# Two-layer encoder trunk on one core: transposes two products behind, a second tile in the attention stream, weight sums of two blocks on VectorE

## The chip, the cores and the metric

The kernel runs on one core of a Trainium2 chip. The metric is the device time of one execution in microseconds. Before the change it took 2719.93 us, the median of three runs (2718.82 to 2721.35).

## What is computed

Two layers over 1024 tokens of 1024 features. Layer 0 mixes tokens by neighbourhood attention, layer 1 by dense differential attention; both go on in the same way:

```python
o = mixer(rms_norm(x, g0))            # attention, then heads side by side
x = x + rms_norm(o @ w_o, g1)         # output projection, 1024 x 1024
u = rms_norm(x, g2) @ w_in            # 1024 x 5632
gate, val = jnp.split(u, 2, axis=-1)
gate = conv1d(gate, conv_w, width=3, per_feature=True) + conv_b
x = x + rms_norm((gelu(gate) * val) @ w_out, g3)
```

and each layer ends with a gated embedding that is added to x. In differential attention each head has two softmaxes, w = a0 - lam a1, and the head's output is normalised (`os` in the kernel) before w_o.

## The kernel before

**Products.** A float32 operand is split into a high part and a low part, each rounded for TensorE, and a product is three matmuls: high by high, high by low, low by high. The split of a loaded `raw` page into its parts is an activation on ScalarE (line 135) for the high part and a subtraction on VectorE (line 138) for the low one. A tile of 128 tokens times w_o is 8 steps over k, each 3 matmuls for each half of 512 columns: 48 matmuls of 128x512 (line 816).

**Order.** TensorE's instructions stand in the order in which the code emits them. The order of ScalarE, VectorE, GpSimd (POOL) and of the DMA queue on SyncE (SP) is made by a scheduler, except in a region from `mix_out`'s last product to the end of `first_three`, where ScalarE's and VectorE's order is the code's too. Each engine works strictly through its own list.

**The stream of layer 1.** `da` runs over 64 pairs of head and tile of queries: scores (line 637), softmax, turns of the weights (`da_turn`, line 659), values (`da_values`, line 673) and the output (`da_out`): the normalised `os` (line 679; a chain ScalarE line 676, VectorE line 677, POOL line 184, VectorE line 679) is transposed by one matmul (line 687). Between these steps `tick` lets a generator, `qkv_stream`, put in matmuls of other work: the qkv projections of later heads, then the first tile of the output projection (`first_out`, in two `pj` banks, k = 0 to 6, since k = 7 needs the last head). `last_rows` lays out the jobs that load and split w_o and the first tile's rows. `drain` runs what is left of the stream.

**`mix_out`.** Tiles go in the order 0, 4, 1, 5, 2, 3, 6, 7. For each: the product into one of two PSUM pages `m`; squares on ScalarE into the page `h` (line 956), the root on VectorE and POOL (lines 960, 184), the scaled residual (lines 966, 969), the norm (lines 179, 180, 192, into `h` again), and then on TensorE 8 transposes of `h` in two banks (line 203), which `put` copies and splits into the operand pages of the next stage. In iteration n TensorE has product n, then the transposes of tile n-1, written Tn-1 here (T0 to T7 by place in that order). The last product, T6, the first product of `gated` and T7 follow in the region; the last norm is line 1006.

**`gated`.** The product with w_in is made in 22 blocks of 128 features, each by a seven-product scheme on quarters: `one`, `six`, `two`, `five`, `three`, `four`, `seven`, 12 matmuls each. It needs four sums of the block's weight quarters (S1 to S4, `Block.sum`, line 1147, 128x512) and after the products sums out of PSUM on VectorE: `sum_u` (line 1174, must precede `three`, which goes on in the same bank), `upper` (line 1186, must precede `seven`), `sum_on`, `lower`. `c` is line 1180, ScalarE's copy, which must precede `four`; the second half of `upper` runs on POOL (line 1189). `taps` (line 1098), `gelu` and `mult` (line 1214, the two halves of c times v) end a block, and c and its sums are spilled to memory. Blocks 0 to 2 run in `first_three`, whose order is written by hand; from block 3 on the loop below it runs, with S1 to S4 on POOL.

**Who feeds whom.** SP issues all loads and spills in order; a load of weight quarters needs a free `raw` page (three), a spill needs its data.

Of the kernel before, what the change touches and what calls it, by code (L numbers as in the profile page):

```python
# [8 lines left out]
F32 = mybir.dt.float32  # L9
# [7 lines left out]
P = 128  # L17
D = 1024
SEQ = 1024
NT = SEQ // P  # L20
KT = D // P
# [5 lines left out]
D_HEADS = 8  # L27
FT = 22
PK = 2
EPS = 1e-6  # L30
LAMBDA_INIT = 0.8 - 0.6 * math.exp(-0.3)
RPITCH = 31
# [59 lines left out]
class Trunk:  # L92
# [229 lines left out]
    def qkv_stream(self, layer, hT, x, first, mid):  # L322
# [3 lines left out]
        W = self.i["qkv"][layer]  # L326
# [89 lines left out]
        self.last_rows(layer)  # L416
        yield from emb
        yield from self.first_out()

    def begin(self, stream):  # L420
        self.stream, self.qk, self.v, self.credit = stream, {}, {}, 0.0
# [276 lines left out]
    def da(self, hT, oT, first, mid):  # L698

        N = NT * D_HEADS  # L700
        with self.tc.tile_pool(name="xa1", bufs=2, reuse_waits="tile") as x, \
             self.psum("s", 2) as self.ps:
            self.begin(self.qkv_stream(1, hT, x, first, mid))
            self.chunk = {}
            self.need(self.qk, 0)
            self.da_scores(x, 0)
            self.tick(12 / 6)
            for n in range(N + 1):
                if n > 0:
                    self.need(self.v, (n - 1) // NT * 2 + 1)  # L710
                    self.da_values(x, n - 1)
                if n + 1 < N:
                    self.need(self.qk, (n + 1) // NT)
                    self.da_scores(x, n + 1)
                if n < N:
                    self.da_turn(x, n, 0)
                self.tick(0.34)
                if n < N:
                    self.da_turn(x, n, 1)
                self.tick(0.16)  # L720
                if n > 0:
                    self.da_out(x, n - 1, oT)
                self.tick(0.5)
            self.drain()

    def psum(self, name, bufs):
        return self.tc.tile_pool(name=self.uid("ps" + name), bufs=bufs, space=PSUM, reuse_waits="tile")
# [17 lines left out]
    def last_rows(self, layer):  # L745


        nc = self.nc
        src = self.i[("na_w_o", "da_w_o")[layer]]
        self.W, self.part0 = [], None  # L750
        page = lambda dt=F32R: self.page(self.r1, "r1", (P, 4, D), dt)
        pages = [page(), page(), page(F32)]
        raw = {}

        def load(kt):
            if kt < 4:
                raw[kt] = pages[2][:, kt]
            else:
                raw[kt] = self.page(self.raw, "raw")
            nc.sync.dma_start(raw[kt], src[kt * P : kt * P + P])  # L760

        def row(kt):
            if kt == 4:
                del pages[2]
                pages.extend([page(), page()])
            hi, lo = pages[2 * (kt // 4) : 2 * (kt // 4) + 2]
            parts = hi[:, kt % 4], lo[:, kt % 4]
            did = self.split(raw.pop(kt), *parts)
# [12 lines left out]
        for kt in range(6):  # L781
            load(kt)
        self.jobs += [lambda kt=kt: row(kt) for kt in range(6)] + [part, None] + [lambda kt=kt: row(kt) for kt in (6, 7)]

    def job(self, act, dve):

# [49 lines left out]
    def first_out(self):  # L836
# [9 lines left out]
        self.row(KT - 1)  # L846
        self.out0 = hi, lo, m

    def mix_out(self, layer, x_in, x1):


# [7 lines left out]
        with self.tc.tile_pool(name=f"xb{layer}", bufs=2, reuse_waits="tile") as x, self.psum("m", 2) as pm:  # L859
            W, last = self.W, self.opage  # L860
            order = (0, 4, 1, 5, 2, 3, 6, 7)
            b12, b21, b22 = (self.page(xl, k, (P, 4, 512)) for k in ("B12", "B21", "B22"))

            def load_x(t):
# [7 lines left out]
                return hi, lo, xi or load_x(t)  # L872

            with self.tc.manual_schedule(engines={ENG.SP}):
                second = self.out_part(layer, order[1])
                xs = [load_x(order[0])]
                g1 = self.bcast(x, "g1", self.i["norm_g"][layer, 1], bufs=1)
                xs.append(load_x(order[1]))
                g2 = self.bcast(x, "g2", self.i["norm_g"][layer, 2], bufs=1)
            hs = [self.page(x, "h"), self.page(x, "h")]  # L880
# [53 lines left out]
                        sum_t3(t), sum_t4(t, t2)  # L934
                return of_group

            def product_of(n, t):
                hi, lo, xi = ready.pop(0)
                part = [(hi[:, k], lo[:, k]) for k in range(KT)]
                h = hs[n] if n < 2 else self.page(x, "h")  # L940
                if n >= 2:
                    hs.append(h)
                if t == 0:
                    m = self.out0[2]
                    self.times(m, part[KT - 1 :], W[KT - 1 :], first=False)
                else:
                    m = pm.tile([P, D], F32, tag="m", name=self.uid("m"))
                    m = [m[:, :512], m[:, 512:]]
                    self.times(m, part, W)
                return m, h, xi  # L950

            def squares(m, h):
                ss = [self.col("ss"), self.col("sy")]
# [17 lines left out]

            ready = [load(*a) for a in zip(order, xs, (self.out0[:2], second))]
            for n, t in enumerate(order[:-1]):
                m, h, xi = product_of(n, t)
                residual(t, m, h, xi, root_of(squares(m, h)))
                self.normed(xi, h, g2)
                if n + 2 < NT:
                    ready.append(load(order[n + 2]))
                if n > 0:
                    self.transposed(hs[n - 1], put(order[n - 1], hs[n - 1]))  # L980
            gate = self.gate_begun(layer, X)

# [96 lines left out]
    def gated(self, layer, X, spill, spare):  # L1079
# [38 lines left out]
        with self.tc.tile_pool(name=f"xd{layer}", bufs=1, reuse_waits="tile") as y, self.psum("c", 2) as pc:  # L1118
# [7 lines left out]
            class Block:  # L1126
# [82 lines left out]
                def gelu(b):  # L1209
                    act(b.c, b.c, AF.Gelu_apprx_tanh)  # L1210

                def mult(b):
                    for n in (1, 0):
                        tt(out=halves(b.c)[n], in0=halves(b.c)[n], in1=wide(b.v[:, 512 * n : 512 * n + 512]), op=ALU.mult)

            def first_three():
# [531 lines left out]
```

## Time and profile before

| | |
|---|---|
| median of 3 runs | 2719.93 us |
| profiled execution | 2720.59 us |
| its span | 2718.8 us |
| TensorE's granted clock, mean | 0.999 |
| TensorE busy | 2680.8 us (99%) |
| VectorE / ScalarE / POOL busy | 71% / 49% / 17% |
| `mix_out` of layer 0 / layer 1 | from about 480 / 1894 us |
| `gated` of layer 0 / layer 1 begins | 551 / 1979 us |

Durations are microseconds; PE is TensorE, PEld its weight loads, DVE VectorE, ACT ScalarE. Waits are idle time of an engine and what ended it. A row of the timeline is: start, length, engine, line, operation, out<-in, shape, count, and in brackets the idle time before it with its releaser. A row of the windows is: stretch, length, then busy time of PE, PEld, DVE, ACT and POOL (with counts), the granted clock, the DMA share and GB/s.

### The profile page before, as it was taken

The page shows a single profiled execution, that of the slowest core. Times are in us where ns is not written, and L with a number is a line of the kernel's source. Part 1 is how long each engine was busy: PE and PEld are TensorE (multiplying, and loading weights), DVE is VectorE, ACT ScalarE, POOL GpSimd, SP SyncE. Part 2 cuts the span into 40 slices and gives each one's busy share as a digit, 9 for nine tenths or more (in the row PEclk, how much of TensorE's full clock was granted, in tenths as well). Part 3 has the DMA queues.
Part 4 walks back from the last instruction along what each step waited for, and adds up shares of the span by engine and source line. Part 5 has one row for each costly group of instructions (what it writes and reads, how often), then busy time and mean ns, then how long its engine had stood idle before and what let it go on. Part 6 is the DMA issues. An engine that isn't in the chain of part 4 may idle for free.

```text
span 2718.8 us, 36612 instructions
## 1 busy us (share of the span) xinstructions
PE 2680.8 (99%) x13492; PEld 2218.4 (82%) x13492; DVE 1938.8 (71%) x3318; ACT 1319.7 (49%) x2469; POOL 462.6 (17%) x461
## 2 busy tenths in 40 slices
PE   8999999999999999999999999999999999999999
PEld 6888887877888888888888888877877888888887
DVE  5777776689777767676566666676688777767674
ACT  5555556454444444454455555555454344444452
POOL 2221210014333300001000000000014333300000
PEclk9999999999999999999999999999999999999999
DMA  6223226413332373433211111124323333374342
GB/s 183 84 67 105 73 93 200 134 63 121 111 108 102 109 275 123 116 132 113 77 46 47 45 47 46 54 77 143 129 67 115 114 105 105 103 262 135 116 138 98
DMA packets 129334, 297.97 MB, mean 110 GB/s; under 512 B 11737, under 2 KB 37721, under 8 KB 129154
## 3 DMA queue, kind: packets, MB, share of 16 engines
q1 hardware_dynamic: 129154, 295.63, 33.0%
q8 instruction: 106, 1.74, 0.3%
q14 instruction: 74, 0.61, 0.1%
HBM read 221.17 MB, written 86.61 MB: 113 GB/s over the span
## 4 chain that ended last, share of the span: by engine, by line
PE 90%; DVE 5%; ACT 2%; DMA 1%; issue 1%; POOL 0%; SPq 0%; ACTq 0%; POOLq 0%; DVEq 0%
PE b L172 20%; PE b L173 20%; PE b L174 20%; PE g L816 6%; PE m L816 5%; PE b L673 4%; PE s L637 4%; PE b L659 2%; PE b L203 2%; PE b L816 2%; PE av L533 2%; PE b L506 1%; DVE r L138 1%; PE s L487 1%; PE s L486 1%
## 5 line engine op out<-in xcount | busy, mean ns | idle before, releaser
L172 PE MATMUL b<-r,ws 128*128 128x512 f32 (+1 forms) x1344 | 548.2, 408 | 5.6 <-DVE u L1174 3.9
L173 PE MATMUL b<-r,ws 128*128 128x512 f32 (+1 forms) x1344 | 520.0, 387 | 0.6 <-DVE r L138 0.5
L174 PE MATMUL b<-r,ws 128*128 128x512 f32 (+1 forms) x1344 | 520.4, 387 | 0.0
L172 PEld LDWEIGHTS b<-r,ws 128*128 128x128 f32 x1344 | 254.2, 189 | 54.6 <-DVE u L1174 5.2
L174 PEld LDWEIGHTS b<-r,ws 128*128 128x128 f32 x1344 | 253.5, 189 | 53.0
L173 PEld LDWEIGHTS b<-r,ws 128*128 128x128 f32 x1344 | 255.0, 190 | 36.5 <-DVE r L138 1.9
L172 PE MATMUL b<-r,wa 128*128 128x512 f32 x688 | 268.5, 390 | 4.8 <-DVE B L1186 3.7
L466 ACT ACTIVATE E<-E,mn 128x1024 f32<-128x1024 f32 (+2 forms) x256 | 221.5, 866 | 102.0 <-DVE mn L462 101.7
L172 PE MATMUL b<-r,r 128*128 128x512 f32 x680 | 268.9, 395 | 1.3 <-ACT ws L1534 1.0
L174 PE MATMUL b<-r,wa 128*128 128x512 f32 x688 | 268.1, 390 | 0.0
L173 PE MATMUL b<-r,wa 128*128 128x512 f32 x688 | 267.9, 389 | 0.0
L173 PE MATMUL b<-r,r 128*128 128x512 f32 x680 | 265.5, 390 | 0.1
L174 PE MATMUL b<-r,r 128*128 128x512 f32 x680 | 265.2, 390 | 0.0
L184 POOL TENSOR_TENSOR ss<-ss,mhalf 128x1 f32<-128x1 f32 x128 | 75.9, 594 | 1098.3 <-DVE ss L677 558.8
L138 DVE TENSOR_TENSOR ws<-raw,ws 128x512 fp32r<-128x512 f32 (+3 forms) x168 | 170.2, 1020 | 52.3 <-ACT ws L135 51.4
L135 ACT ACTIVATE r<-raw 128x512 fp32r<-128x512 f32 (+1 forms) x168 | 110.6, 665 | 192.9 <-PE b L173 169.9
L135 ACT ACTIVATE ws<-raw 128x512 fp32r<-128x512 f32 (+3 forms) x168 | 124.3, 748 | 124.0 <-PE b L174 52.1
L138 DVE TENSOR_TENSOR r<-raw,r 128x512 fp32r<-128x512 f32 (+1 forms) x168 | 126.8, 760 | 70.6 <-ACT r L135 67.4
L816 PE MATMUL m<-r,ws 128*128 128x512 f32 x672 | 157.1, 393 | 0.0
L172 PEld LDWEIGHTS b<-r,wa 128*128 128x128 f32 x688 | 129.2, 188 | 33.5 <-DVE B L1186 5.3
L816 PE MATMUL g<-r,ws 128*128 128x512 f32 x672 | 155.8, 391 | 0.0
L462 DVE CUSTOM_DVE_ANT_0 E<-s,T 128x1024 f32<-128x1024 f32 x128 | 151.1, 1217 | 4.1 <-PE s L637 4.1
(188 smaller groups left out, 5096.6 us busy)
## 6 DMA issues: line engine op xcount, KB each, us to landing
raw<-in_w_in SPq DMA_DIRECT2D x86, 512.0 KB, 3.5
raw<-in_qkv SPq DMA_DIRECT2D x48, 512.0 KB, 5.7
spillS<-r SPq DMA_DIRECT2D x88, 256.0 KB, 3.2
r<-in_ffn_w_out SPq DMA_DIRECT2D x40, 512.0 KB, 6.3
raw<-spillS SPq DMA_DIRECT2D x40, 512.0 KB, 3.6
spillA<-B SPq DMA_DIRECT2D x66, 256.0 KB, 2.9
raw<-spillA SPq DMA_DIRECT2D x30, 512.0 KB, 3.9
x<-x SPq DMA_DIRECT2D x24, 512.0 KB, 3.5
```

The costliest lines, as they stand in the source:

```text
L135: return self.nc.scalar.activation(hi, src, AF.Copy).ins
L138: return self.nc.vector.tensor_tensor(out=lo, in0=src, in1=hi.bitcast(F32), op=ALU.subtract).ins
L172: mm(out, sta[0], mov[0], start=first, stop=False, skip_group_check=onto)
L173: mm(out, sta[0], mov[1], start=False, stop=False, skip_group_check=onto)
L174: mm(out, sta[1], mov[0], start=False, stop=last, skip_group_check=onto)
L184: self.nc.gpsimd.tensor_tensor(out=ss, in0=ss, in1=self.mhalf, op=ALU.pow)
L203: self.nc.tensor.transpose(t[:, k * P : k * P + P], h[:, c : c + P], self.ident)
L462: nc.vector.tensor_tensor_reduce(out=e, in0=s, in1=bias, scale=1.0, scalar=3e38, op0=ALU.add, op1=ALU.min, accum_out=mn)
L466: self.exp = nc.scalar.activation(e, e, AF.Exp, bias=mn, scale=-1.0, accum_out=sm).ins
L637: nc.tensor.matmul(s[m][:, w], A[o, a, q], A[o, b, w], start=z == 0, stop=z == 2)
L673: nc.tensor.matmul(o, wT[:, k], V[:, k], start=k == 0, stop=k == KT - 1)
L816: mm(out[half], a, b[:, w], start=first and k + z == 0, stop=last and k == n - 1 and z == 2)
```

## The change

It has four parts.

1. In `mix_out` the transposes of a tile come after the product two tiles on: in iteration n TensorE has product n, then Tn-2. The last product is cut after its third k step; T5 stands in the cut and T6 behind it. From the third tile on, the page `h` of tile n is asked for only after Tn-2's `put` (the pool has two).
2. In layer 1 the second tile's operand (t = 4) is split in the stream by one more job, and 7 of the 8 k steps of its product run in the stream (`second_out`). Its output is a page of the stream's own PSUM pool, which `mix_out` takes over; layer 0 opens a pool of the same kind. 0.6 of a tick stands ahead of the last values and `drain` behind them, ahead of the last output.
3. In `first_three`, the half 1 of block 0's `mult` stays ahead of block 2's `three` and `upper`, half 0 comes behind them.
4. S1 to S4 of blocks 3 and 4 are made on VectorE: 16 instructions in the two layers.

The core of the diff:

```diff
+        if layer == 1:
+            yield from self.second_out()
...
-        with self.tc.tile_pool(name="xa1", bufs=2, reuse_waits="tile") as x, \
-             self.psum("s", 2) as self.ps:
+        self.spool = self.psum("s", 2)
+        self.ps = self.spool.__enter__()
+        with self.tc.tile_pool(name="xa1", bufs=2, reuse_waits="tile") as x:
...
             for n in range(N + 1):
+                if n == N:
+                    self.tick(0.6)
                 if n > 0:
                     self.need(self.v, (n - 1) // NT * 2 + 1)
                     self.da_values(x, n - 1)
...
+                if n == N:
+                    self.drain()
                 if n < N:
                     self.da_turn(x, n, 0)
...
-            self.drain()
...
+        if layer == 1:
+            def second():
+                self.part1 = self.out_part(layer, SECOND)
+                return self.did
+
+            self.part1 = None
+            self.jobs += [None, second]
...
+    def second_out(self):
+
+        while self.part1 is None:
+            self.hurry()
+        hi, lo = self.part1
+        m = self.ps.tile([P, D], F32, tag="s", name=self.uid("m"))
+        m = [m[:, :512], m[:, 512:]]
+        yield from self.times_steps(m, [(hi[:, k], lo[:, k]) for k in range(KT - 1)], self.W, last=False)
+        self.out1 = hi, lo, m
...
-                if t == 0:
-                    m = self.out0[2]
+                if t == 0 or layer == 1 and n == 1:
+                    m = (self.out1 if n else self.out0)[2]
                     self.times(m, part[KT - 1 :], W[KT - 1 :], first=False)
                 else:
-                    m = pm.tile([P, D], F32, tag="m", name=self.uid("m"))
+                    m = self.ps.tile([P, D], F32, tag="s", name=self.uid("m"))
                     m = [m[:, :512], m[:, 512:]]
-                    self.times(m, part, W)
+                    if amid is None:
+                        self.times(m, part, W)
+                    else:
+                        for _ in self.times_steps(m, part[:3], W[:3], last=False):
+                            pass
+                        amid()
+                        self.times(m, part[3:], W[3:], first=False)
...
-                m, h, xi = product_of(n, t)
+                m, xi = product_of(n, t)
+                if n > 1:
+                    self.transposed(hs[n - 2], put(order[n - 2], hs[n - 2]))
+                    hs.append(self.page(x, "h"))
+                h = hs[n]
                 residual(t, m, h, xi, root_of(squares(m, h)))
...
-                if n > 0:
-                    self.transposed(hs[n - 1], put(order[n - 1], hs[n - 1]))
...
-            m, h, xi = product_of(NT - 1, b)
+            m, xi = product_of(NT - 1, b, lambda: self.transposed(hs[-2], put(order[-3], hs[-2])))
+            h = self.page(x, "h")
...
-                b0.mult()
+                b0.mult((1,))
                 b2.three(), b2.upper(), b2.upper_on(pool)
+                b0.mult((0,))
...
-                        b.sum(s, pool)
+                        b.sum(s, tt if f < 5 else pool)
```

TensorE at the end of layer 1's stream, before: the last values (line 673) and the transpose of `os` stand next to each other; the rows on b ahead of and behind them are the first tile's product in its two banks.

```order
L816 MATMUL b_2748_16671<-r_2682_16391,ws_16487 128x512
L673 MATMUL b_2770_16805<-v_15918,wT_16774 128x128 x8
L687 MATMUL b_2770_16805<-ident,os_16814 128x128
L816 MATMUL b_2747_16670<-r_2682_16391,ws_16486 128x512
L816 MATMUL b_2748_16671<-r_2682_16391,ws_16486 128x512
```

And after (line numbers of the changed kernel are higher: 830 for 816, 676 for 673, 690 for 687): `m_16811` is the second tile's page, its rows being matmuls in pairs of halves.

```order
L830 MATMUL m_16811<-r_2633_16183,ws_16729 128x512 x2
L676 MATMUL b_2774_16824<-v_15918,wT_16780 128x128 x8
L830 MATMUL m_16811<-r_2633_16183,ws_16728 128x512 x2
...
L830 MATMUL m_16811<-r_2682_16391,ws_16729 128x512 x2
L690 MATMUL b_2774_16824<-ident,os_16833 128x128
L830 MATMUL b_2747_16670<-r_2682_16391,ws_16486 128x512
```

15 rows of the second tile, 30 matmuls, now stand between the last values and the transpose of `os`, and 12 stand ahead of the values.

VectorE in layer 0's `gated`, ahead of block 2's `upper` (line 1186), before: the operands `wa` of block 2 and both halves of block 0's `mult` (line 1214).

```order
L138 TENSOR_TENSOR wa_6001<-r_1037_5617,wa_6001 128x512
L138 TENSOR_TENSOR wa_6004<-raw_5890,wa_6004 128x512
L1214 TENSOR_TENSOR B_949_4941<-B_949_4941,B_947_4939 128x16x32 x2
L1186 TENSOR_TENSOR B_947_4939<-b_1075_5962,B_948_4940 128x512
L1098 SCALAR_TENSOR_TENSOR B_949_4941<-u_5752,convw,B_949_4941 128x15x32
```

And after (139 for 138, 1250 for 1214, 1222 for 1186; 1183 is `Block.sum`, 1147 before):

```order
L139 TENSOR_TENSOR wa_6001<-r_1037_5617,wa_6001 128x512
L139 TENSOR_TENSOR wa_6004<-raw_5890,wa_6004 128x512
L1183 TENSOR_TENSOR r_1037_5617<-raw_6106 128x512
L1183 TENSOR_TENSOR r_1037_5617<-raw_6104,raw_6106 128x512
L1250 TENSOR_TENSOR B_949_4941<-B_949_4941,B_947_4939 128x16x32
L1183 TENSOR_TENSOR r_1037_5617<-r_1037_5617,raw_6104 128x512
L1222 TENSOR_TENSOR B_947_4939<-b_1075_5962,B_948_4940 128x512
L1250 TENSOR_TENSOR B_949_4941<-B_949_4941,B_947_4939 128x16x32
```

Three sums of block 3 now stand ahead of that `upper`, and one half of `mult` has moved behind it.

ScalarE in layer 0's `mix_out` around the squares of the tile of place 6 (line 956, `h_5457`), before: only one split of a gate operand stands between the norm of the tile of place 5 (line 179) and them.

```order
L135 ACTIVATE B_948_4940<-b_1019_5449 128x64x8
L179 ACTIVATE h_5367,ss_5427<-x_5254 128x1024
L135 ACTIVATE ws_5541<-raw_5537 128x512
L956 ACTIVATE h_5457,ss_5507<-m_5458 128x512
L956 ACTIVATE h_5457,sy_5508<-m_5458 128x512
```

And after (136 for 135, 988 for 956, 180 for 179; the page is `h_5506`):

```order
L136 ACTIVATE ws_5526<-raw_5522 128x512
L180 ACTIVATE h_5416,ss_5427<-x_5254 128x1024
L136 ACTIVATE ws_5529<-raw_5522 128x512
L136 ACTIVATE r_942_4926<-b_1019_5491 128x64x8
L136 ACTIVATE r_944_4928<-b_1020_5498 128x64x8
L988 ACTIVATE h_5506,ss_5507<-m_5442 128x512
```

The squares have moved behind the second gate split and behind two copies out of T4's banks.

More of the change, by code (lines that the diff above doesn't have):

```diff
@@ L29 @@
 PK = 2
+SECOND = 4
 EPS = 1e-6
@@ L858, in mix_out @@
         xl = self.xl.__enter__()
-        with self.tc.tile_pool(name=f"xb{layer}", bufs=2, reuse_waits="tile") as x, self.psum("m", 2) as pm:
+        with ExitStack() as pools:
+            x = pools.enter_context(self.tc.tile_pool(name=f"xb{layer}", bufs=2, reuse_waits="tile"))
+            if layer == 0:
+                self.ps = pools.enter_context(self.psum("s", 2))
+            else:
+                pools.push(self.spool)
             W, last = self.W, self.opage
-            order = (0, 4, 1, 5, 2, 3, 6, 7)
+            order = (0, SECOND, 1, 5, 2, 3, 6, 7)
             b12, b21, b22 = (self.page(xl, k, (P, 4, 512)) for k in ("B12", "B21", "B22"))
@@ L874, in mix_out @@
             with self.tc.manual_schedule(engines={ENG.SP}):
-                second = self.out_part(layer, order[1])
+                second = self.out_part(layer, order[1]) if layer == 0 else self.out1[:2]
                 xs = [load_x(order[0])]
@@ L935, in put, with product_of @@
                 return of_group
-            def product_of(n, t):
+            def product_of(n, t, amid=None):
                 hi, lo, xi = ready.pop(0)
                 part = [(hi[:, k], lo[:, k]) for k in range(KT)]
-                h = hs[n] if n < 2 else self.page(x, "h")
-                if n >= 2:
-                    hs.append(h)
-                if t == 0:
-                    m = self.out0[2]
+                if t == 0 or layer == 1 and n == 1:
+                    m = (self.out1 if n else self.out0)[2]
                     self.times(m, part[KT - 1 :], W[KT - 1 :], first=False)
                 else:
-                    m = pm.tile([P, D], F32, tag="m", name=self.uid("m"))
+                    m = self.ps.tile([P, D], F32, tag="s", name=self.uid("m"))
                     m = [m[:, :512], m[:, 512:]]
-                    self.times(m, part, W)
-                return m, h, xi
+                    if amid is None:
+                        self.times(m, part, W)
+                    else:
+                        for _ in self.times_steps(m, part[:3], W[:3], last=False):
+                            pass
+                        amid()
+                        self.times(m, part[3:], W[3:], first=False)
+                return m, xi
             def squares(m, h):
@@ L986, in mix_out @@
             a, b = order[-2:]
-            m, h, xi = product_of(NT - 1, b)
+            m, xi = product_of(NT - 1, b, lambda: self.transposed(hs[-2], put(order[-3], hs[-2])))
+            h = self.page(x, "h")
+            hs.append(h)
             (a1, a2), (b1, b2) = sums(hs[-2]), sums(h)
@@ L1210, in gelu, with mult @@
                     act(b.c, b.c, AF.Gelu_apprx_tanh)
-                def mult(b):
-                    for n in (1, 0):
+                def mult(b, parts=(1, 0)):
+                    for n in parts:
                         tt(out=halves(b.c)[n], in0=halves(b.c)[n], in1=wide(b.v[:, 512 * n : 512 * n + 512]), op=ALU.mult)
```

## The prediction

> **What bounds the kernel now.** I read the page first (shares of the engines), then TensorE's waits within the two stretches that the change touches, then the timelines of those places.
>
> ```profile
> PE 2680.8 (99%) x13492; PEld 2218.4 (82%) x13492; DVE 1938.8 (71%) x3318; ACT 1319.7 (49%) x2469; POOL 462.6 (17%) x461
> ```
>
> TensorE is busy for 2680.8 of 2718.8 us and the change leaves its instructions as many as they were, so only the 38 us of holes can be won. The profiled execution took 2720.6, its span 2718.8; the median of the runs is 2719.9, 0.7 below the profiled one. TensorE's waits in layer 0 from 480 to 700 us (columns: us in total, times, longest) are
>
> ```profile
> PE b L172 <- DVE B L1186: 2.7, 2, 2.3
> PE b L172 <- DVE u L1174: 1.7, 2, 1.0
> PE b L203 <- DVE h L1006: 1.2, 1, 1.2
> PE b L203 <- DVE h L192: 0.7, 2, 0.4
> PE b L172 <- ACT c L1180: 0.3, 1, 0.3
> ```
>
> and in layer 1 from 1840 to 2130 us
>
> ```profile
> PE b L172 <- DVE u L1174: 2.2, 1, 2.2
> PE b L687 <- DVE os L679: 1.9, 1, 1.9
> PE b L172 <- DVE B L1186: 1.0, 1, 1.0
> PE b L172 <- ACT c L1180: 0.8, 1, 0.8
> PE b L659 <- ACT wT L662: 0.7, 1, 0.7
> PE b L203 <- DVE h L192: 0.7, 2, 0.4
> PE b L816 <- ACT ws L1534: 0.6, 1, 0.6
> ```
>
> The L172 rows stand in `gated`, blocks 2 to 4; the L203 rows on h L192 are transposes of `mix_out`; the others are the end of layer 1's stream. A wait costs more than its idle time. Around the longest one in layer 0:
>
> ```profile
> 608.66 0.39 PE L174 MATMUL b<-r,wa 128*128 128x512 f32 x1
> 611.33 0.50 PE L172 MATMUL b<-r,wa 128*128 128x512 f32 x1 [2.28 <-DVE B L1186]
> 611.66 0.39 PE L173 MATMUL b<-r,wa 128*128 128x512 f32 x1
> 1931.44 10.94 PE m L816 x48
> ```
>
> 48 matmuls in 10.94 are 0.227 apart. From 608.66 to 611.66 there are 3.00 for two steps of 0.227, so 2.55 was lost where the idle column says 2.28: about 0.27 on top of each wait. In `gated` that makes 2.7+1.7+0.3 + 5 x 0.27 = 6.0 in layer 0 and 2.2+1.0+0.8 + 3 x 0.27 = 4.8 in layer 1: 10.8 is the most that the last two edits can give.
>
> **Weight sums on VectorE, and the split `mult`.** VectorE is what these waits end on, and it has no slack there, but some of its time is lost beside POOL:
>
> ```profile
> 600.00:610.00 10.00, 9.04 (x40) 7.14 (x39) 10.00 (x12) 7.58 (x12) 6.16 (x4) 1.00 0.29 102
> 599.46 0.69 DVE L1147 TENSOR_TENSOR r<-raw,r 128x512 f32<-128x512 f32 x1
> 600.06 0.69 DVE L1174 TENSOR_TENSOR u<-b,B 128x512 f32<-128x512 f32 x1
> 603.91 1.69 DVE L138 TENSOR_TENSOR wa<-r,wa 128x512 fp32r<-128x512 f32 x1
> 605.52 1.78 DVE L138 TENSOR_TENSOR wa<-raw,wa 128x512 fp32r<-128x512 f32 x1
> 607.22 3.45 DVE L1214 TENSOR_TENSOR B<-B,B 128x512 f32<-128x512 f32 x2
> 610.60 0.68 DVE L1186 TENSOR_TENSOR B<-b,B 128x512 f32<-128x512 f32 x1
> 645.60 1.29 DVE L1214 TENSOR_TENSOR B<-B,B 128x512 f32<-128x512 f32 x2 [0.66 <-ACT B L1210]
> L1147 POOL TENSOR_TENSOR r<-raw,r 128x512 f32<-128x512 f32 x38 | 51.1, 1345 | 25.4 <-DVE wa L138 25.1
> ```
>
> From 600 to 610 VectorE (the figure behind PE and PEld) is busy for all 10.00. The same 128x512 subtraction takes 0.69 (next start after 0.60) when POOL is quiet and 1.69 or 1.78 from 603.91 on, where POOL makes its sums; the two halves of `mult` take 3.45 there and 1.29 later. So a sum on POOL, 1.345 long, costs a VectorE operation beside it about 1.05, and the same sum on VectorE costs 0.60. For 8 sums a layer: 8 x 0.60 = 4.8 added, up to 8 x 1.05 = 8.4 taken away.
>
> The Trainium skill, page "SBUF — State Buffer", section "SBUF: two separate sides", calls this an exclusive lock between GpSimd and a VectorE operation with two SBUF inputs, where the loser waits out the whole other instruction. An estimate by that rule from POOL's 1.345 would be a relief of 8 x 1.345 = 10.8 a layer; the excess of 1.00 to 1.09 above is less than a whole instruction, and I go by it.
>
> Laid out by the new order in layer 0 from 603.91: two wa (1.2), two sums (1.2), one half of `mult` (0.65), one sum (0.6), so the upper sum B of block 2 starts at 607.6 and ends at 608.3, where it started at 610.60. TensorE would ask for it at 608.66 + 0.23 = 608.9: the wait of 2.28 goes. Going on in the same way, the operand u of block 3's third product is ready at about 621.3 and asked for at 622.5 (626.27 less the waits up to there); c of block 3 is early too. What is late next: upper of block 3 ends at about 628.6 where TensorE now asks at 627.9, a wait of 0.95 with its surcharge, since VectorE was given eight sums before it; and u of block 4, 0 to 1.1, taken as 0.5, because block 5's sums on POOL fall beside it. Layer 0: 6.0 - 0.95 - 0.5 = 4.5. Layer 1 has the same order and less to lose: its three waits go, about 0.6 stays at block 3: 4.2. Together 8.7. Bounds: half of the relief (8 x 0.5 = 4.2 against 4.8 added) leaves the edit to the `mult` that moves behind upper, which alone takes 0.65 to 1.7 from that chain; I take 5.0 for that end and 10.5 for the other.
>
> SP is passed as well. The load of block 4's quarters now stands behind the spill A11 of block 0's c, which waits for the later half of its `mult`:
>
> ```profile
> 611.16 0.37 SPq L1063 DMA_DIRECT2D raw<-in_w_in  x1
> raw<-in_w_in SPq DMA_DIRECT2D x86, 512.0 KB, 3.5
> ```
>
> In before it went out at 611.16; now the half is done at 609.1 and the slot free when the fourth sum of block 3 is done at 612.2, so it lands at about 615.8, 2 us before VectorE wants it. Nothing.
>
> **The second tile in layer 1's stream.** Its end in before:
>
> ```profile
> 1868.37 0.95 ACT L135 ACTIVATE ws<-raw 128x896 fp32r<-128x896 f32 x1 [2.28 <-DMA pp<-ws]
> 1884.01 1.63 PE L816 MATMUL b<-r,ws 128*128 128x512 f32 x6
> 1888.35 1.95 PE L673 MATMUL b<-v,wT 128*128 128x128 f32 x16
> 1891.76 0.41 DVE L679 TENSOR_SCALAR os<-b,sum,ss 128x128 f32<-128x128 f32 x1 [0.73 <-POOL ss L184]
> 1892.23 0.33 PE L687 MATMUL b<-ident,os 128*128 128x128 f32 x1 [1.93 <-DVE os L679]
> 1892.32 2.12 PE L816 MATMUL b<-r,ws 128*128 128x512 f32 x6
> 1893.00:1897.00 4.00, 4.00 (x13) 3.10 (x12) 1.61 (x4) 2.30 (x6) 0.55 (x1) 0.57 0.44 164
> 1894.44 12.02 PE m L816 x48
> ```
>
> After the last values (1888.35 + 1.95) TensorE has nothing until ACT, VectorE, POOL and VectorE again have made os: 1.93 idle, 2.18 with its surcharge. In the new order 30 matmuls of the second product (6.8 us) stand there, and the chain of 1.9 is hidden. These 30, with the 12 ahead of the values, are taken out of a product that TensorE made later in before: work moved at no price.
>
> Right behind that wait the granted clock (third figure from the end) is 0.57: the six matmuls take 2.12 where six take 1.63, and the 48 take 12.02 where they take 10.94, so 0.49 + 1.08 = 1.57 lost. I count it as gone with the wait. The 1.93 is too short to be sure of that: waits of 2.2 and 2.3 in `gated` are followed by a clock of 1.00:
>
> ```profile
> 611.00:615.00 4.00, 3.67 (x16) 3.06 (x17) 4.00 (x7) 1.66 (x3) 1.63 (x1) 1.00 0.65 201
> ```
>
> The Trainium skill, page "TensorE: Matmul & The Clock Gate", section "The two states you'll see" of its part on the clock, has the half clock follow an idle window of about 3.4 us; by that rule this 1.93 would not be the cause, and the half clock would stay somewhere. That is a rival below.
>
> The two ACT waits before it (wT 0.7, ws 0.6, with surcharge 1.8) come from one place: ACT stood from 1868.37 for 0.95 on a ws split, after 2.28 on its DMA. The job is now asked for elsewhere and the split lies behind the exps, so 0.95 of 1.8 comes back; the rest is the hand-over of the next row. Stream: 2.18 + 1.57 + 0.95 = 4.7. Bounds: only the os wait, 2.0; all, 5.5. The 42 matmuls themselves stood in `mix_out` and cost nothing new. Product 3's bank comes free 0.5 before it is wanted, its operands 0.35 before: covered, thinly, and in the lower bound.
>
> **Transposes two products on.**
>
> ```profile
> 538.95 0.59 ACT L956 ACTIVATE h<-m 128x512 f32<-128x512 f32 x1
> 541.36 1.41 DVE L966 SCALAR_TENSOR_TENSOR h<-m,ss,g 128x512 f32<-128x512 f32 x2
> 547.25 1.28 DVE L192 SCALAR_TENSOR_TENSOR h<-x,ss,g 128x1024 f32<-128x1024 f32 x1 [0.73 <-POOL ss L184]
> ```
>
> A tile's chain, from squares to h, takes 547.25 + 1.28 - 538.95 = 9.6; the product that covers it takes 10.9, and two tiles a layer still miss by 0.35. Those four waits, 4 x (0.35 + 0.17) = 2.1 (0.17 is what the row at 611.33 lost ahead of its first matmul), go: with two products (23 us) between a product and its transposes they cannot be missed. But the last tiles have less. T6 stands behind T4, 18 matmuls, T5 and 30 matmuls: 0.8 + 4.1 + 0.8 + 6.8 = 12.5 after product 6, and its squares now stand behind the put of T4 on ACT: two ws splits, the L179 of tile n = 5 and two copies out of T4's banks, estimated at 3 from the 0.59 of a 128x512 activation (twice that for L179). 3.0 + 9.6 = 12.6, and the chain also meets the put of T5 on VectorE (0.7, one such operation): ready at 13.3, a new wait of 0.8 in each layer. The wait on h L1006 (T7, 1.2) stays, since its chain stands behind T6's. Sum: 2.1 - 1.6 = +0.5. Bounds: no new wait, +2.1; twice that wait, -1.1. The bank of product n+2 is wanted 12.6 after product n and free at 3 + 541.36 + 1.41 - 538.95 = 6.8: it does not bind.
>
> **The sum.** 8.7 + 4.7 + 0.5 = 13.9 off 2720.6 gives 2706.7 for a profiled execution, 2706.0 by the median. The worst ends, 5.0 + 2.0 - 1.1 = 5.9, give 2714.0; the best, 10.5 + 5.5 + 2.1 = 18.1, 2701.8. A measurement of this kernel tells 0.2% (5.4 us) from no change.
>
> **The rivals.**
>
> *VectorE stays the bound in `gated`.* For it: 10.00 of 10.00 busy; against it: the 1.69 and 3.45 rows. With half of the relief, 4 of the 8.7 come: 2711 (0.18). With none of the 8.7, 5.2 in all: 2714.7, no change by the bound above (0.12).
>
> *The half clock stays, and T6 waits for longer.* The 1.57 turns up behind another wait or at no wait (the clock page's rule would allow that, as the 1.93 is short of its window), and T6 waits 3.0 instead of 0.8 in both layers as its chain meets more on VectorE: 13.9 - 1.6 - 4.4 = 7.9, 2712 (0.07). With the clock alone, 2707.6, inside the forecast.
>
> *Slower: the sums themselves meet POOL.* POOL keeps its halves of upper (line 1189) in blocks 2 to 4, and a sum on VectorE reads two SBUF operands like the wa rows. If each takes 1.73 with no relief elsewhere, 16 x 1.73 = 27.7 lands on a VectorE without slack, and 2720.6 - 5.2 + 27.7 = 2743. It decides from (5.2 + 5.4) / 16 = 0.66 us of net cost a sum; its bare 0.60 stays below, and the relief above speaks against it (0.04).
>
> That the change doesn't do what it says is out: the order of the instructions shows all four edits.
>
> **The numbers.** The forecast, 2701.5 to 2709, has 0.59; the two cases at 2711 and 2712 have 0.25, no change 0.12, slower 0.04: faster 0.84. The range takes in the first two: 2701.5 to 2714.5.
>
> **What would show it.** Right: no wait on os at the end of layer 1's stream and a clock of 1.00 behind it; no wait of blocks 2 and 3 on upper or u over 1 us; wa rows near 0.69 around 604; L203 waits on h L192 only at T6, below 1 us. Wrong: a VectorE still full with u of block 3 or 4 late by 2 us, sums of 1.7 on VectorE, or a product of `mix_out` waiting for its bank or operands.

## The result and the profile after

The changed kernel took 2705.78 us, the median of four runs (2705.19 to 2706.55), where the kernel before took 2720.51 in its four: a ratio of 0.9947 (95% interval 0.9932 to 0.9961), 14.7 us less. The forecast was 2706.0. The profiled execution took 2705.19, its span is 2703.4, 15.4 below the span before: 10.2 of that is idle time of TensorE, and 5.2 is time in which it counted as busy.

The page's first row and TensorE's waits, whole, from 480 to 700 in layer 0 and from 1835 to 2120 in layer 1 (lines of the changed kernel are higher: L1222 is `upper`, L1042 the last norm, L830 the output projection, L1571 the stream's `ws`):

```profile
PE 2675.6 (99%) x13492; PEld 2216.0 (82%) x13492; DVE 1938.2 (72%) x3334; ACT 1320.1 (49%) x2469; POOL 437.4 (16%) x445
```

```profile
PE b L173 <- DVE B L1222: 1.4, 2, 1.2
PE b L204 <- DVE h L1042: 1.2, 1, 1.2
PE b L174 <- DVE r L139: 0.2, 1, 0.2
PE b L204 <- ACT B L136: 0.2, 1, 0.2
```

```profile
PE b L204 <- DVE h L1042: 1.2, 1, 1.2
PE b L830 <- ACT ws L1571: 0.6, 1, 0.6
PE b L173 <- DVE B L1222: 0.6, 1, 0.6
PE b L173 <- ACT ws L1571: 0.4, 2, 0.3
PE b L174 <- DVE r L139: 0.2, 1, 0.2
PE b L204 <- ACT B L136: 0.2, 1, 0.2
```

The waits on u, c, os, wT and h L192 are gone; of `upper` 1.4 and 0.6 are left, and a new small wait on a copy of ScalarE (ACT B) is there once a layer. The waits on the last norm (1.2 in each layer), on r (0.2 in each layer) and of `gated` on ws (0.5 in layer 1) were there before too.

Where the time went can be read stage by stage, because TensorE has 13492 instructions in both traces and the n-th of them does the same work in both outside the moved stretches. The difference of its start, after less before, grows like this (the row of 472 lies within the first product of `mix_out` that is made whole there, 467.8 to 478.8, so that layer 0's `mix_out` begins some 12 us ahead of the 480 in the table of before):

| up to (us of before) | difference, sum | of this stage | forecast |
|---|---|---|---|
| first product of `mix_out`, layer 0 (472) | -0.45 | -0.45 | 0 |
| first product of `gated`, layer 0 (551) | -1.01 | -0.56 | -0.25 |
| block 4 of `gated`, layer 0 (660) | -5.10 | -4.09 | -4.5 |
| late in layer 1's stream (1868) | -5.49 | -0.39 | 0 |
| first product of `gated`, layer 1 (1979) | -10.84 | -5.35 | -4.95 |
| block 4 of `gated`, layer 1 (2073) | -15.30 | -4.46 | -4.2 |
| end of the span | -15.42 | -0.12 | 0 |

The stages that the change does not touch add up to -0.96 here; the traces of the experiments are up to 1.0 ahead of or behind before after the first 25 us alone, so that one pair of traces can't tell such a figure from nothing.

VectorE ahead of block 2's `upper` in layer 0, the place where before had 1.69, 1.78 and 3.45:

```profile
602.90 0.68 DVE L139 TENSOR_TENSOR wa<-r,wa 128x512 fp32r<-128x512 f32 x1
604.10 0.68 DVE L1183 TENSOR_TENSOR r<-raw 128x512 f32<-128x512 f32 x1
606.88 0.68 DVE L1222 TENSOR_TENSOR B<-b,B 128x512 f32<-128x512 f32 x1
631.43 2.88 DVE L1250 TENSOR_TENSOR B<-B,B 128x512 f32<-128x512 f32 x2
636.04 1.78 DVE L1353 TENSOR_TENSOR r<-B 128x512 f32<-128x512 f32 x1
```

The operands take 0.68 or 0.69 each, a sum the same, and `upper` starts at 606.88, 3.7 earlier than before, of which 1.0 was won ahead of this stage. From 631 on, beside the sums of block 5 on POOL, the long rows are back.

### The profile page after: what moved, and what is told of

It is laid out like the page before. It is cut to its first block, busy times and chain, and to the rows that moved or that the text cites. A ratio compares the mean times of both kernels' runs of the same rounds, so it can differ in the third digit from the quotient of the medians.

```text
span 2703.4 us, 36590 instructions
## 1 busy us (share of the span) xinstructions
PE 2675.6 (99%) x13492; PEld 2216.0 (82%) x13492; DVE 1938.2 (72%) x3334; ACT 1320.1 (49%) x2469; POOL 437.4 (16%) x445
## 4 chain that ended last, share of the span: by engine, by line
PE 92%; DVE 4%; DMA 2%; ACT 2%; issue 1%; POOL 0%; SPq 0%; ACTq 0%; POOLq 0%; DVEq 0%
PE b L173 21%; PE b L174 21%; PE b L175 21%; PE g L830 6%; PE m L830 5%; PE b L676 4%; PE s L640 4%; PE b L662 2%; PE b L204 2%; PE b L830 2%; PE av L536 2%; PE b L509 1%; DMA x<-in_x 1%; PE s L490 1%; PE s L489 1%
## 5 line engine op out<-in xcount | busy, mean ns | idle before, releaser
L830 PE MATMUL m<-r,ws 128*128 128x512 f32 x672 | 156.4, 391 | 0.0
L830 PE MATMUL g<-r,ws 128*128 128x512 f32 x672 | 155.8, 391 | 0.0
```

Of the source, the lines that this page charges most:

```text
L830: mm(out[half], a, b[:, w], start=first and k + z == 0, stop=last and k == n - 1 and z == 2)
```

## The experiments

Differences are to the kernel before, run beside them on the same chip (medians 2720.2 for `gated`, `sums`, `mult` and `turn`, 2721.1 for `f4`, `f6`, `stream` and `drain`, 2721.0 for `echo`, `first`, `nosecond` and `early`); by that measure the changed kernel stands at -14.7.

**Parts 3 and 4, together and alone.** `gated` has both:

```diff
-                        b.sum(s, pool)
+                        b.sum(s, tt if f < 5 else pool)
-                b0.mult()
+                b0.mult((1,))
                 b2.three(), b2.upper(), b2.upper_on(pool)
+                b0.mult((0,))
```

> Parts 3 and 4 together in the kernel before, the attention stream and mix_out as before. Theory: the two stages of gated give what they give in the changed kernel, 4.1 in layer 0 and 4.5 in layer 1: 8.6 us below before. Rival (the stages help each other, so parts 1 and 2 are needed): under 6 us.

`sums` has the first of these edits only, `mult` the other.

> Part 4 alone in the kernel before: S1 to S4 of blocks 3 and 4 on VectorE, nothing else. Theory (a sum on POOL costs a VectorE operation beside it 1.05, on VectorE it costs 0.60, so VectorE is ahead earlier): the waits of gated on upper, u and c fall from 10.8 to 2 to 4 in both layers together, time 7 to 9 us below before. Rival (VectorE is full, so what is added to it is on the path): the waits grow, time 3 to 10 us above before.

> Part 3 alone in the kernel before: half 0 of block 0's mult behind block 2's upper. Theory: block 2's upper starts 1.7 earlier in layer 0 (half of the 3.45), so the wait of 2.28 there falls to about 0.6, but VectorE has as much to do as before and is full, so the next waits (u and upper of block 3) take most of it back: time 0 to 2 us below before. Rival (the moved half is what the gain comes from): 4 us or more below before.

Measured: `gated` 2711.33 (ratio 0.9968, 0.9955 to 0.9981), -8.9; `sums` 2711.43 (0.9968, 0.9956 to 0.9980), -8.8; `mult` 2719.02 (0.9996, 0.9987 to 1.0006), -1.2 and no difference by its interval. In `gated` the two stages of the table give -4.3 and -4.5 without any help of the other parts. The sums alone bring nearly all of it, and moving half of `mult` brings nothing that can be told from none by the medians. (In one pair of traces `gated` gains 1.0 more in layer 0 than `sums`, -4.3 against -3.3; the medians, 0.1 apart, don't show it.) TensorE's waits in layer 0 from 600 to 700, of `sums`:

```profile
PE b L172 <- DVE B L1186: 1.9, 3, 1.3
```

and of `mult`:

```profile
PE b L172 <- DVE u L1174: 2.3, 2, 1.7
PE b L172 <- ACT c L1180: 0.8, 1, 0.8
PE b L172 <- ACT B L1165: 0.7, 1, 0.7
PE b L172 <- DVE B L1186: 0.4, 1, 0.4
```

In `mult` the wait of 2.28 on `upper` is gone and is paid on u, c and a new one: 4.2 in all where before had 4.7. On this full VectorE the new order shifted the wait; `sums`, which lightens VectorE's load, took most of it away.

**How many blocks.** `f4` is the changed kernel with `f < 4` in that line, `f6` with `f < 6`.

> The changed kernel with block 4's sums back on POOL (only block 3's on VectorE). Theory: four VectorE operations beside these sums take about 1.05 more while 4 x 0.60 is saved, so block 3's upper is about 1.8 later and its wait grows in both layers: 2 to 4 us above the changed kernel. Rival (block 3's sums alone do it): no difference.

> The changed kernel with block 5's sums on VectorE too. By the rows of the changed kernel the operations beside block 5's sums on POOL lose about 3.2 and four sums cost 2.4: the wait of 1.15 at block 4's upper in layer 0 falls by about 0.8, layer 1 is as it was: 0.5 to 1.5 us below the changed kernel. Rival (VectorE has taken all it can): 1 to 3 us above.

Measured: `f4` 2712.09, -9.0, so 5.7 above the changed kernel; `f6` 2706.25, -14.9, the same as the changed kernel. `f4` is a clean look at the price. Its VectorE while POOL makes block 4's four sums (616.1 to 622.5):

```profile
616.51 1.43 DVE L139 TENSOR_TENSOR wa<-r,wa 128x512 fp32r<-128x512 f32 x1
617.87 1.77 DVE L139 TENSOR_TENSOR wa<-raw,wa 128x512 fp32r<-128x512 f32 x1
619.57 1.78 DVE L139 TENSOR_TENSOR ws<-raw,ws 128x512 fp32r<-128x512 f32 x1
621.27 2.38 DVE L1250 TENSOR_TENSOR B<-B,B 128x512 f32<-128x512 f32 x2
```

0.75, 1.09, 1.10 and 1.10 more than the same operations cost alone (0.68, the pair 1.28): 4.0 for four sums, 1.0 each, as the forecast had it (1.05). TensorE then waits in layer 0

```profile
PE b L173 <- DVE B L1222: 2.3, 1, 2.3
PE b L173 <- DVE u L1210: 1.5, 1, 1.5
```

The stages grow by 2.6 in layer 0 and 3.2 in layer 1 (read up to 2080 of before, as its last wait on u lies behind 2073). That is about the measured 5.7, and more than the 2 to 4 in all that was expected, since u as well as `upper` comes late. With block 5's sums moved too (`f6`) the waits on `upper` in layer 0 fall from 1.4 to 0.8, about as expected, but a new one of 1.0 comes in layer 1, on ScalarE (ACT B), so that neither the 0.5 to 1.5 below nor the rival's 1 to 3 above was measured.

**The contention by itself.** `echo` leaves the sums on VectorE and adds, after each, two POOL additions into a page that nothing reads:

```diff
                         b.sum(s, tt if f < 5 else pool)
+                        if f < 5:
+                            for w in (slice(0, 256), slice(256, 512)):
+                                pool(out=echo, in0=flat(b.at(s))[:, w], in1=flat(b.at(s))[:, w], op=add)
```

> The changed kernel, and after each of the 16 sums on VectorE the same additions are made on POOL too, in two halves of 256 columns, into a page that nothing reads; VectorE's order is that of the changed kernel. Theory (VectorE operations with two SBUF operands lose about 1.05 beside such an addition): up to 8.4 a layer on a VectorE that is full there, less what slack it has: 8 to 16 us above the changed kernel, wa rows at 1.7. Rival (what a sum costs VectorE on POOL is small, the gain was the order): under 2 us.

Measured: 2715.28 (0.9980, 0.9971 to 0.9990), -5.7, so 9.0 above the changed kernel though nothing in its trace waits for an added addition. POOL and VectorE in one stretch of it:

```profile
609.51 5.21 POOL L1332 TENSOR_TENSOR echo<-r 128x256 f32<-128x256 f32 x5
```

```profile
612.13 1.10 DVE L139 TENSOR_TENSOR wa<-r,wa 128x512 fp32r<-128x512 f32 x1
613.15 1.10 DVE L1357 TENSOR_TENSOR r<-B 128x512 f32<-128x512 f32 x1
614.18 1.10 DVE L139 TENSOR_TENSOR wa<-r,wa 128x512 fp32r<-128x512 f32 x1
615.20 0.68 DVE L139 TENSOR_TENSOR ws<-raw,ws 128x512 fp32r<-128x512 f32 x1
```

While POOL runs, each VectorE row starts 1.02 after the one ahead of it and takes 1.10; as soon as POOL stops it is 0.68. Rows of 1.7 did not come, as the additions were half as wide: the loss went with the width of POOL's instruction. In the trace the two stages lose 4.8 and 4.4 against the changed kernel; up to 1.7 of the first is a stretch of half clock behind a wait of 3.25 on `upper`. So what POOL's additions take from VectorE is large enough to make a gain of 8.7, and the rival that the added sums would weigh on a full VectorE falls.

**Transposes alone.** `turn` has part 1 only; the core of it, against the kernel before:

```diff
                 m, xi = product_of(n, t)
+                if n > 1:
+                    self.transposed(hs[n - 2], put(order[n - 2], hs[n - 2]))
...
-                if n > 0:
-                    self.transposed(hs[n - 1], put(order[n - 1], hs[n - 1]))
```

> Part 1 alone: transposes two products on, in both layers; stream, mult and sums as before (layer 1's mix_out still takes the stream's pool). Theory: the four waits on h L192 go (2.1), a wait of about 0.3 at T5's second group comes in each layer: 1.0 to 1.5 us below before, no wait at T6. Rival (T6 waits for its chain by 0.8 or more in each layer): 0.5 below to 1 above.

Measured: 2719.34 (0.9998, 0.9989 to 1.0008), -0.9: no difference by its interval, though the trace has the four waits gone and -0.57 in layer 0's `mix_out`, as in the changed kernel. It also has two stretches of half clock where that of before has one (last section).

**The second tile alone.** `stream` has part 2 only. Against the changed kernel parts 3 and 4 are taken out, and part 1 so that transposes come one product on:

```diff
                 m, xi = product_of(n, t)
-                if n > 1:
-                    self.transposed(hs[n - 2], put(order[n - 2], hs[n - 2]))
...
+                if n > 0:
+                    self.transposed(hs[n - 1], put(order[n - 1], hs[n - 1]))
```

> Part 2 alone: second tile of layer 1 in the stream, transposes one product on, mult and sums as before. Theory: the wait on os (2.2 with its surcharge), the slow clock behind it (1.6) and the wait on wT (1.0) go: 4.5 to 5 us below before, all of it at the end of layer 1's stream. Rival (the slow clock is not tied to that wait): 3.0 to 3.5.

Measured: 2727.40, slower than before (1.0022, 1.0012 to 1.0031), +6.3. Neither theory had that. TensorE there:

```profile
1899.71 1.52 PE L830 MATMUL m<-r,ws 128*128 128x512 f32 x6
1910.07 1.94 PE L204 MATMUL b<-ident,h 128*128 128x128 f32 x8 [8.84 <-DVE ss L992]
```

At the stream's end it had won 4.8 against before; then T0 waits for 8.84, and three windows of half clock (10.2 us, 1904.5 to 1914.8) lie over that wait and the work behind it: T0 takes 1.94 where it takes 1.03 in the next rows below, and the product behind it 12.65 where others take 11.15. In before T0 follows a product of 48 matmuls. Here 42 of these were made in the stream, T0 follows the six that are left, and tile 0's chain, about 10 long, lies open. `first` tests that: `stream`, with T0 alone moved behind the third product.

```diff
+                if layer == 1 and n == 2:
+                    self.transposed(hs[0], put(order[0], hs[0]))
...
-                if n > 0:
+                if n > layer:
                     self.transposed(hs[n - 1], put(order[n - 1], hs[n - 1]))
```

> Part 2 alone once more, with one thing added: in layer 1 the transposes of the first tile stand behind the third product (48 matmuls) and not behind the second, of which the stream leaves only six; all others one product on. Theory (the 8.8 us at T0 come from its cover having moved into the stream): that wait goes, T1 behind it waits for up to 2: 3 to 5 us below before. Rival (the second tile's bank or operands hold mix_out up): 2 us or more above before, as with part 2 alone.

Measured: 2723.31 (1.0010, 1.0001 to 1.0020), +2.3.

```profile
1899.11 12.41 PE L830 MATMUL m<-r,ws 128*128 128x512 f32 x54
1911.36 1.03 PE L204 MATMUL b<-ident,h 128*128 128x128 f32 x8
1917.47 1.94 PE L204 MATMUL b<-ident,h 128*128 128x128 f32 x8 [5.07 <-DVE h L193]
```

T0's wait is gone, so its cover was what was missing and no bank or operand held it up; but T1 waits for 5.07 in place of the 2 that I allowed, and takes 1.94, again at half clock. Both tiles end within 2 us of each other and their chains run one behind the other on ScalarE and VectorE: T1 can start at 1917.47, 17 after tile 1's last matmul (the sixth of the 54, at about 1900.5), and one product of 11 does not cover two chains. Two products on, T0 and T1 stand behind products 2 and 3. So part 1, which alone can't be told from no change, is what makes part 2 pay.

**Part 2 on top of the others.** `nosecond` is the changed kernel without part 2 (no second tile in the stream, drain behind the last output).

> The changed kernel without part 2: parts 1, 3 and 4. Theory: the waits on os and wT come back, the slow clock may or may not: 3.0 to 5.0 us above the changed kernel. Rival (part 2 is worth as little with part 1 as alone): no difference or below it.

Measured: 2709.37 (0.9961, 0.9946 to 0.9976), -11.6: 3.1 above the changed kernel. The waits on os (1.9) and wT (0.9) are back, with no slow clock behind them in its trace.

**What covers os.** `drain` and `early` move the same 42 matmuls.

```diff
@@ drain
-                if n == N:
-                    self.tick(0.6)
...
-                if n == N:
-                    self.drain()
...
+            self.drain()
@@ early
                 if n == N:
-                    self.tick(0.6)
+                    self.drain()
...
-                if n == N:
-                    self.drain()
```

> The changed kernel with drain put back behind the last output and the tick of 0.6 taken out: the second tile's split and product stay in the stream, but nothing of it is kept for the time in which os is made. Theory: the wait on os comes back with about 2, and a stretch at a clock near half behind it costs 1.6: 3.5 to 4 us above the changed kernel. If the slow clock is no matter of that wait, the wait alone: 2.0 to 2.5 us above, the granted clock 1.00 behind it.

> The changed kernel with all 42 matmuls of the second tile ahead of the last values (drain in place of the tick of 0.6), so that nothing stands between the values and the transpose of os. Theory: the wait on os comes back with 1.9, 2.2 with its surcharge; by the runs so far the clock behind it is slow in some programs and 1.00 in others with the same wait, so it is 2 to 4 us above the changed kernel, and the granted clock tells which. Rival (os is hidden by something else): no difference.

Measured: `drain` 2705.36, -15.8, not to be told from the changed kernel; `early` 2708.92, -12.1, 2.6 above it. My expectation for `drain` was wrong: the ticks that stand between values and output in any case put ten matmuls of the second tile there.

```profile
1882.22 1.95 PE L676 MATMUL b<-v,wT 128*128 128x128 f32 x16
1883.92 2.53 PE L827 MATMUL m<-r,ws 128*128 128x512 f32 x10
1886.30 0.27 PE L690 MATMUL b<-ident,os 128*128 128x128 f32 x1
```

Ten matmuls are 2.3 us, just over the chain of 1.9; the other 30 stand behind. In `early`, where nothing stands between them, the wait is back at its full size:

```profile
1890.83 1.95 PE L676 MATMUL b<-v,wT 128*128 128x128 f32 x16
1894.71 0.33 PE L690 MATMUL b<-ident,os 128*128 128x128 f32 x1 [1.94 <-DVE os L682]
1894.80 1.63 PE L828 MATMUL b<-r,ws 128*128 128x512 f32 x6
```

The six matmuls behind it take 1.63, full speed; its trace grows by 2.1 here. Its four runs are spread over 2706.8 to 2711.3. One stretch of half clock, 3.41 long, costs 1.7 at most, so it can't make that spread alone; what does is not shown.

## Why the prediction was right, point by point

*The bound.* Right in the main: with TensorE's list unchanged the time fell by what its waits cost, 14.7 (15.4 in the traces) for a sum of 13.9. But "only the 38 us of holes can be won" is too narrow: 5.2 of the 15.4 came off the busy time, as the surcharge on a wait and the half clock count as busy.

*Weight sums and `mult`.* Forecast 4.5 and 4.2; the stages gave 4.1 and 4.5. The mechanism is shown from both sides (`f4`, `echo`). Two details were off. What is late next is `upper` of block 4 in layer 0, 1.15, where I had put 0.5 on its u, and 0.27 at block 3's in place of 0.68. And the split of `mult`, which I used in laying out VectorE's order and in the lower bound, is worth nothing that the medians show: `sums` does without it. That lower bound of 5.0 does not follow from its terms either: half of 1.05 for 8 sums is 4.2 (8 x 0.5 would be 4.0) against 4.8 added, and 0.65 to 1.7 from `mult` is 3.4 at most in two layers.

*The lock.* I went by the row, 1.05 an operation, against 1.345 that the estimate from the Trainium skill's page "SBUF — State Buffer", section "SBUF: two separate sides", gave. `f4` has 1.0 a sum: the measurement stays with the row, and is less than the whole instruction that the section has the loser wait for. That POOL's work alone slows VectorE, as that section has it, is what `echo` shows.

*The stream.* Forecast 4.7. The os wait went and so did wT, ws stayed at 0.6, and the stream's end gave 4.8 in the traces. But three steps of it were right for less than I said. That 30 matmuls hide the chain is true; ten do. And "the 42 matmuls themselves stood in `mix_out` and cost nothing new" holds only beside part 1: alone they cost 11 us there (`stream`: 4.8 won, 6.3 lost in the end). I had costed each part apart and did not ask what the moved matmuls had been hiding. The third is the half clock.

*The half clock.* Counted at 1.57 as the price of the os wait. In the traces of before and `turn`, six matmuls behind that wait take 2.12 and 2.51; in `gated`, with the same idle time, they take 1.64 (`turn` first):

```profile
1891.85 2.51 PE L823 MATMUL b<-r,ws 128*128 128x512 f32 x6
```

```profile
1888.27 1.64 PE L816 MATMUL b<-r,ws 128*128 128x512 f32 x6
```

So it is a risk that a wait of this size brings, not its price. Of the seven traces in which the os wait stands open, three have it (before, `mult`, `turn`) and four don't (`gated`, `sums`, `nosecond`, `early`); the last section shows what decides. That the 4.7 fits a pair of traces is in part luck, since the profile of before happened to be one of the three; by the medians part 2 was worth 3.1 on top of the others (`nosecond`). In which share of the untraced runs of before it fell is not shown; the last section has an estimate. The rival that it would stay elsewhere did not come true: no matmuls at half pace are in the trace of the changed kernel.

*Transposes.* Forecast 0.5 won, with a new wait of 0.8 at T6 in each layer; the trace has 0.56 won in layer 0, and `nosecond` against `gated` 0.57 in layer 1, so 1.1 for both. In the changed kernel (first TensorE, then the h of T6 on VectorE):

```profile
536.19 1.04 PE L204 MATMUL b<-ident,h 128*128 128x128 f32 x8
536.98 4.35 PE L830 MATMUL m<-r,ws 128*128 128x512 f32 x18
541.17 0.60 PE L204 MATMUL b<-ident,h 128*128 128x128 f32 x4
541.92 0.66 PE L204 MATMUL b<-ident,h 128*128 128x128 f32 x4 [0.15 <-ACT B L136]
542.33 7.09 PE L830 MATMUL m<-r,ws 128*128 128x512 f32 x30
549.41 1.07 PE L204 MATMUL b<-ident,h 128*128 128x128 f32 x8
```

```profile
547.98 1.28 DVE L193 SCALAR_TENSOR_TENSOR h<-x,ss,g 128x1024 f32<-128x1024 f32 x1 [0.73 <-POOL ss L185]
```

The chain was sized well: h is there 13.1 after product 6 ended (549.26 less 536.19), forecast 13.3. The cover was mis-sized: T4, 18 matmuls, T5 and 30 matmuls take 13.2 (536.19 to 549.41), not 12.5. T5 takes 1.16 in place of 0.8, with a wait of 0.15 on a copy of ScalarE in it, and the two stretches of matmuls 0.1 and 0.3 more than 0.227 apiece. So the wait moved from T6 to T5, and shrank.

*The rivals.* VectorE as the bound, half or whole, and the sums meeting POOL: against all of them stand `sums` and `echo`. The slower case priced a sum on VectorE at 1.73, beside POOL's halves of `upper`. That did not come: in the changed kernel's trace all 32 rows of `Block.sum` on VectorE take 0.67 to 0.69.

## What to carry to other kernels

Where two engines contend, count the time that moved work takes from its neighbour as well as its own: a POOL addition of 1.3 to 1.7 (`f4`) cost VectorE 1.0, and 0.6 when VectorE made it itself. Before matmuls are moved to fill one hole, ask what they cover where they are now, and price the parts of a change together as well as apart: here part 1 alone couldn't be told from no change, part 2 alone cost 6.3, and the two with the rest gave -14.7. On a full engine an edit of the order may only move a wait, as `mult` did; here it was less contention beside the engine that took the wait away.

## What the runs showed of the hardware

A wait far shorter than 3.4 us can bring a stretch of half clock, and need not; where it falls decides. The traces show this from the granted clock (third figure from the end of a row of the windows).

Up to the last matmul, a stretch of half clock lasts 3.41 us (10.24, three times that, once in `stream`), and stretches of one trace start whole multiples of 3.413 apart: in `mult` at 1892.94, at 2053.37 (47 times) and behind the last matmul at 2715.55 (194 times more). So time is cut into windows of 3.413, and the cut lies elsewhere in each execution. Set to these cuts, the same wait of 1.94 and 1.93 on os, in `turn` and in `gated`:

```profile
1888.91:1892.32 3.41, 1.47 (x12) 1.24 (x11) 0.56 (x2) 0.65 (x3) 0.55 (x1) 1.00 0.39 101
1892.32:1895.73 3.41, 3.41 (x10) 2.65 (x9) 1.21 (x2) 2.37 (x7) 0.00 (x0) 0.50 0.53 211
```

```profile
1886.90:1890.31 3.41, 2.13 (x10) 1.79 (x11) 0.50 (x2) 1.20 (x2) 0.55 (x1) 1.00 0.81 302
1890.31:1893.72 3.41, 3.41 (x17) 2.82 (x16) 2.47 (x5) 1.47 (x6) 0.55 (x1) 1.00 0.25 69
```

In `turn` the wait lies in one window, which leaves TensorE 1.47 busy and 1.94 idle, and the next window has half the clock. In `gated` a cut divides it, 1.28 is the most in one window, and the clock stays at 1.00. Over the 14 traces, up to the last matmul, this holds without exception: each of the nine windows at full clock with 1.87 or more of idle time is followed by half clock, and no window with 1.83 or less is. The two closest are `mult` and `first`:

```profile
2049.96:2053.37 3.41, 1.54 (x7) 1.00 (x6) 3.41 (x4) 1.15 (x2) 3.33 (x3) 1.00 0.24 90
2053.37:2056.78 3.41, 3.41 (x9) 2.65 (x9) 3.41 (x7) 2.22 (x4) 0.23 (x1) 0.50 0.58 162
```

```profile
606.66:610.07 3.41, 1.58 (x7) 0.96 (x6) 3.41 (x3) 1.49 (x3) 2.59 (x2) 1.00 0.46 154
610.07:613.48 3.41, 2.95 (x13) 2.43 (x14) 3.41 (x6) 1.15 (x2) 1.63 (x1) 1.00 0.73 223
```

So in these traces a wait of 1.9 us has to fall almost wholly into one window. If the cut lies at random, that happens in about half of the executions. (This is an estimate from these figures: the wait of 1.93 has 1.48 of room in a window, with 0.06 to 0.10 to spare at either end, together 1.6 of 3.41.) The waits of 2.2 to 2.3 in `gated` run the same risk: before's own trace kept the full clock behind both of its two, while `turn`, `stream` and `mult` (there 1.9) lost it behind u in layer 1. Parts 3 and 4 took that risk away too, which the prediction didn't count.

The Trainium skill, page "TensorE: Matmul & The Clock Gate", section "What's actually happening", has the half clock follow at least one idle window of about 3.4 us, in windows that run freely. The length of the windows and the cut that moves agree with the traces; that a window has to be idle doesn't, as 1.87 of 3.41 was enough here.
